# Sine table on ScalarE's queue, rotary queries first and query splits ahead of value rows in the opening of a latent attention, with a new order of its second list

## The chip, the cores and the metric

One NeuronCore of a Trainium2 chip. The metric is device time in microseconds (us) of one execution, the median of several runs. The engines are TensorE (PE in the profile), VectorE (DVE), ScalarE (ACT), GpSimd (POOL) and SyncE (SP). PEclk is the share of TensorE's full clock that was granted.

## The reference

One step of a hybrid encoder layer for two groups of rows, a prompt (1024) and a sample (32, with 512 cached rows), all in float32. What matters here is branch A, the multi-head latent attention of the prompt: 8 heads, 64 + 32 columns a head for scores.

```python
q = (rms_norm(q_lat, g_q_lat) @ w_uq).reshape(B, T, H_A, NOPE + ROPE)
q_nope = q[..., :NOPE]
q_rope = apply_rope(q[..., NOPE:], cos[:, None, :], sin[:, None, :])
k_nope, v = (c_kv @ w_uk), (c_kv @ w_uv)              # per head
s = (einsum(q_nope, k_nope) + einsum(q_rope, k_rope)) * MLA_SCALE
p = softmax(where(chunk mask, s, NEG))
o_a = einsum(p, v)
merged = sigmoid(g_a) * (o_a @ w_proj_a) + sigmoid(g_b) * (o_b @ w_proj_b)
```

Here `apply_rope` is `concat(x1 * cos - x2 * sin, x2 * cos + x1 * sin)`. `o_b` is the result of branch B (stick-breaking attention), which is done by the time this stage runs.

## The kernel before

Each float32 product is three matmuls on split operands: a tile `X` is held as an upper part (`hi`, L68, on ScalarE: `XH`, or `wh` of a weight) and a remainder (`lo`, L71, on VectorE: `XL`, `wl`), and `mm3` (L75 to L77) forms H·H + L·H + H·L. So nearly every operand of TensorE passes ScalarE first and VectorE second.

The stages follow one another: the combined projection, branch B, the latents (`stage_lat`, to about 572 us), the latent attention (`stage_mla`, to about 850), the merge, the feed-forward. `stage_mla` handles heads in four pairs. A list of tokens, `ORDER_M` for pairs 0 and 1 and `ORDER_N` for pairs 2 and 3, is read by `mla_attend` and gives the order of PE, ScalarE and VectorE in code order. Tokens begin with 0 or 1, the pair within the list: `S` scores (L1612 to L1617, into one of three `s` banks of PSUM), `M`, `m`, `n` row maxima and their scaling (L954 to L959), `E` the exponential (L961), which frees the bank, `R`, `C`, `c` the division by the sum (L966 to L970), `T` transposes (L806), `h`, `v` their splits, `V` products with the values (L820), `o`, `p` the outputs. Other tokens are fillers without a dependence on the scores: `f` is one step (three matmuls) of `o_b @ w_proj_b` (`proj_b`), `G` its store, `U`, `W`, `w` load and split the next weight of that projection, `Y` a step of the sample's attention, `q`, `r` split the last pair's outputs. In the second list the `Y` steps end with transposes (L1787), copied to `os` on VectorE (L1792), stored by GpSimd (L1794) and loaded again by SyncE (L1666) for the merge, whose first matmuls need the split of that load.

The change is mostly in the opening of `stage_mla`, ahead of the first list. Its pieces, by the tokens of `expansion(0)`: `y` the keys' matmuls, `H g L b` their splits into KH and KL; `z` the matmuls of the rotary part of four heads' queries (`rotary`), `B` (`turned`) the product of one third of them with the cosine or sine table (L1476 on VectorE), and behind the last third a store to DRAM on SyncE (L1478: rqc, rqs); `x` the matmuls of the other 64 columns a head, `X` and `K` their copies into a query tile (L1495 on VectorE, L1493 on ScalarE), where the first `X` also issues the loads of the stored products into rows 64 to 127 of the two query tiles (`rows`, L1485 on SyncE); `J` and `j` the query splits QH (L68) and QL (L71), `Z` a copy of the sample's query columns (L1508, L1509). `vstep` gives the values, 12 matmuls a step, with their copies (L1552) and remainders on ScalarE and VectorE in turn. `proj["P"]` fetches four tiles of `o_b` on SyncE (L1826), `proj["O"]` splits them into ObH and ObL. `krope_out` writes out the rotated keys; the rope rows of the keys are split into rows 64 to 127 of KH and KL, and GpSimd copies them to the second head's tiles.

The two tables are loaded at the start of the stage by SyncE (L1417); the sine table's tile is named KSm.

Of the kernel before, what the change touches and what calls it, by code (L numbers as in the profile page):

```python
# [44 lines left out]
class K:  # L45
# [838 lines left out]
    ORDER_N = """  # L884
        0S0.1 0M0.1 0S0.0 0n0.1 f 0M0.0 0S1.1 W f 0E0.1 0S2.0b 0n0.0 0M1.1 0R0.1 0E0.0 f 0R0.0 0c0.0 0C0.1
        0M2.0b 0S2.0a 0T0.0 f 0n1.1 0E1.1 0M2.0a 0m2.0 f w G 0h0.0 0R1.1 f 0v0.0 0E2.0a 0S1.0 0M1.0 f 0E2.0b
        0n1.0 f 0S2.1a 0C1.1 0M2.1a W 0S2.1b f 0M2.1b G 0E1.0 0m2.1 f 0E2.1a f 0S3.0b 0M3.0b 0s2.0 0E2.1b 0R1.0
        w f 0c1.0 0S3.0a f 0M3.0a 0s2.1 0m3.0 0R2.1 0V0.0 0o0 0S3.1b 0M3.1b 0E3.0a 0E3.0b f 0p0 0D 0T1.0 0T1.1
        0R2.0 G 0S3.1a 0h1.1 0M3.1a 0v1.1 f 0m3.1 f 0C2.1 0c2.0 0S4.0b f 0h1.0 0M4.0b f 0v1.0 0E3.1b G 0V1.1
        0s3.0 0E3.1a 0S4.0a 0T2.2 f 0T2.1 0M4.0a 0V1.0 0h2.2 0v2.2 0R3.0 0m4.0 0h2.1 0S4.1b f 0M4.1b 0E4.0b G  # L890
        0o1 0T2.0 f 0p1 0S4.1a 0v2.1 0V2.2 f 0s3.1 0h2.0 f 0E4.0a 0R3.1 0v2.0 0s4.0 f 0C3.1 0V2.1 0c3.0 f 0R4.0
        0V2.0 0T3.2 0o2 0T3.3 G 0M4.1a f3 0m4.1 0h3.2 0p2 0S5.0a f 0h3.3 0E4.1b 0I 0v3.3 0T3.1 0E4.1a 0V3.3
        0S5.0b 0v3.2 0V3.2 0i f 0M5.0b 0h3.1 0c4.0 U f2 G 0T3.0 0M5.0a 0m5.0 0v3.1 0E5.0b 0S5.1b 0h3.0 0x 0s4.1
        0R4.1 0S5.1a 0E5.0a 0C4.1 0x 0x 0T4.3 0M5.1b W 0M5.1a 0V3.1 0v3.0 G 0S6.1 0m5.1 0s5.0 0X 0R5.0 0h4.3
        0E5.1b 0T4.2 0v4.3 w 0E5.1a 0x 0V3.0 0h4.2 0T4.1 U 0M6.1 0s5.1 0R5.1 0x 0K 0o3 0h4.1 0x 0v4.2 0C5.1 0p3
        0x 0v4.1 0c5.0 0x 0K 0n6.1 0x 0V4.3 0V4.2 0E6.1 0T4.0 0X 0S6.0 0K 0T5.2 0S7.0 0h4.0 0X 0y 0R6.1 0Z 0J 0Z
        0C6.1 0M6.0 0h5.2 0v4.0 0n6.0 0E6.0 0y 0j 0R6.0 0V4.1 0V4.0 0H 0T5.1 0M7.0 0o4 0h5.1 0v5.2 0n7.0 0T5.0
        0S7.1 0L 0p4 1S1.0 0h5.0 0V5.2 0v5.1 0c6.0 0M7.1 0g 0J 0E7.0 0v5.0 0b 1M1.0 0j 0n7.1 f 0V5.1 0V5.0 0R7.0
        0T6.1 0T6.0 0o5 0h6.1 1S0.0 0y f 0c7.0 0v6.1 f2 0y G f 0h6.0 0H 0g 0E7.1 W 1S0.1 f2 1n1.0 1E1.0 f 1S2.0b
        1Y G 0v6.0 0R7.1 0C7.1 1M0.1 0p5 0L 0V6.1 1M0.0 1n0.1 1n0.0 0T7.0 1E0.0 1Y 1E0.1 1S2.0a w 0h7.0 1M2.0b  # L900
        1Y 1M2.0a 1R0.0 1m2.0 0V6.0 1Y 1c0.0 1S1.1 0b 1R0.1 0o6 1M1.1 1E2.0b 1Y 1E2.0a 1C0.1 0p6 1S2.1b 0v7.0
        0V7.0 1n1.1 1Y 1R1.0 1T0.0 1M2.1b 1S2.1a f 1M2.1a 1E1.1 1R1.1 1Y 1s2.0 0o7 1h0.0 1m2.1 1E2.1b f 1c1.0
        0p7 1Y 1C1.1 1R2.0 1v0.0 1E2.1a 1s2.1 1Y 1V0.0 f 1c2.0 1o0 1T1.1 1R2.1 1h1.1 1T1.0 1Y f 1h1.0 1C2.1
        1S3.0b 1v1.1 f 1p0 1T2.1 1M3.0b 1S3.0a 1v1.0 1M3.0a G U 1m3.0 f 1h2.1 1V1.1 1S3.1a 1E3.0a 1V1.0 1E3.0b
        1Y 1S3.1b 1v2.1 1M3.1a 1T2.2 1h2.2 f2 1o1 1T2.0 1M3.1b 1v2.2 1m3.1 f 1E3.1a 1Y 1p1 1Y 1S4.0b 1E3.1b
        1s3.0 1s3.1 1S4.0a 1M4.0b 1Y 1h2.0 f 1R3.0 1M4.0a 1Y 1c3.0 1q 1S4.1b 1V2.2 1M4.1b 1m4.0 1E4.0a 1Y 1E4.0b
        1R3.1 1Y 1v2.0 1S4.1a W 1C3.1 1Y 1M4.1a 1r 1m4.1 1T3.3 1q 1V2.1 1V2.0 1h3.3 1Y 1s4.0 1o2 1E4.1a 1R4.0
        1E4.1b 1Y 1v3.3 w 1T3.2 1h3.2 1r G 1s4.1 1R4.1 1p2 1Y 1v3.2 1T3.1 1V3.3 1V3.2 1T3.0 1c4.0 1h3.1 f 1Y
        1C4.1 f 1Y 1S5.0a 1S5.0b 1h3.0 1v3.1 1T4.3 1v3.0 1V3.1 1V3.0 1M5.0b 1M5.0a f 1q 1h4.3 1o3 1v4.3 1m5.0
        1T4.2 1S5.1b 1p3 1T4.1 1Y 1h4.2 1V4.3 1v4.2 1E5.0b 1h4.1 1S5.1a 1v4.1 1V4.2 1E5.0a 1M5.1b 1T4.0 1Y 1S6.1  # L910
        1h4.0 1M5.1a 1V4.1 1Y f 1m5.1 1s5.0 1M6.1 1r 1Y 1E5.1b G 1Y 1n6.1 1R5.0 1E5.1a 1s5.1 1v4.0 1c5.0 1S6.0
        1Y 1R5.1 1E6.1 1C5.1 1q 1M6.0 1T5.2 1R6.1 1Y 1n6.0 1h5.2 1V4.0 1C6.1 1r 1o4 f 1v5.2 1T5.1 1E6.0 1R6.0
        1h5.1 1p4 f 1v5.1 1T5.0 1S7.0 1c6.0 1M7.0 1n7.0 1S7.1 1V5.2 1h5.0 1v5.0 1T6.1 1V5.1 1q 1h6.1 1V5.0 G
        1M7.1 1v6.1 1o5 1T6.0 f 1E7.0 1h6.0 1n7.1 1Y 1r 1p5 1R7.0 1V6.1 1E7.1 1c7.0 f 1v6.0 1V6.0 1o6 1R7.1
        1C7.1 1T7.0 1h7.0 1p6 f3 1q 1v7.0 f G 1r 1q 1V7.0 f 1o7 1Y f 1p7 G 1r 1q 1r
    """.split()
# [493 lines left out]
    def stage_mla(self):  # L1410
# [4 lines left out]
        tc_, ts_ = M.tile([P, T], F32, name="tc", bufs=1), self.tl(M, [P, 2 * KS], F32, "KSm")[:, :T]  # L1415
        for x, d in zip((tc_, ts_), self.rtd):
            nc.sync.dma_start(x, d)  # L1417
# [7 lines left out]
        def expansion(p, banks="mm"):  # L1425
# [55 lines left out]
            def rows():  # L1481
                for e in range(2):
                    qf[e] = self.tl(self.At, [P, BIG], F32, "big")
                    for r, d in zip((64, 96), self.rqd):
                        nc.sync.dma_start(qf[e][r : r + 32], d[2 * p + e])  # L1485

# [327 lines left out]
    def proj_b(self, M, AB):  # L1814
# [6 lines left out]
        def fetch():  # L1821
            h = done[0] // 6
            for k in range(4):
                f = self.tl(self.At, [P, BIG], F32, "big") if h else self.tl(self.At, [P, TP], F32, "A")
# [1 line left out]
                self.fetched = nc.sync.dma_start(fs[-1], self.obd[k][:, h * HC : h * HC + HC]).ins  # L1826

# [878 lines left out]
```

## Time and profile before

| | us |
|---|---|
| median of 3 runs (lowest, highest) | 1706.3 (1703.85, 1706.9) |
| the profiled execution | 1706.11 |
| its span in the profile | 1704.3 |
| TensorE busy | 1648.0 |
| VectorE busy | 1268.7 |
| ScalarE busy | 1008.8 |

The profiled execution's own time and its span differ by 1.8 us. Rows of a timeline give the start in us from the span's start, the duration, engine, line, operation, out<-in with its tile, and in brackets the idle time before it and what ended it. SPq is SyncE's queue of DMA issues. A row of the windows gives, for a stretch, the busy time (and count) of PE, PEld (weight loads), DVE, ACT and POOL, then the granted clock, the DMA share and GB/s. A row of the waits gives who waited for what: total us, times, the longest.

### The profile page before, as it was taken

The numbers are of one execution on the slowest core, as the hardware profiler recorded it, in microseconds if no ns is written. First come the engines' busy times: TensorE is split into PE (matmuls) and PEld (weight loads), VectorE is DVE, ScalarE is ACT, GpSimd is POOL, SyncE is SP. The second block draws the span as 40 slices with busy tenths as digits, with TensorE's granted clock in tenths as the row PEclk, the third lists the DMA queues.
The fourth block names the chain that finished last, engine by engine and source line by source line (L and its number), as shares of the span: only waits on it lengthen the run. The fifth ranks groups of instructions, "written<-read, shape, count | busy, mean of one in ns | idle before, by whom it ended". The sixth has DMA issues, their size and how long they took to land. (4 is left out here: it accounts for less than half of the span.)

```text
span 1704.3 us, 30277 instructions
## 1 busy us (share of the span) xinstructions
PE 1648.0 (97%) x11592; PEld 1512.1 (89%) x11592; DVE 1268.7 (74%) x2140; ACT 1008.8 (59%) x1945; POOL 303.9 (18%) x581
## 2 busy tenths in 40 slices
...
GB/s 357 102 112 197 276 240 163 171 189 185 163 111 64 145 93 92 105 65 35 112 248 137 180 124 63 144 104 132 128 107 135 130 103 135 228 328 247 207 139 121
DMA packets 194145, 260.62 MB, mean 153 GB/s; under 512 B 23374, under 2 KB 132304, under 8 KB 193936
## 3 DMA queue, kind: packets, MB, share of 16 engines
...
q10 hardware_dynamic: 224, 0.09, 0.0%
...
## 5 line engine op out<-in xcount | busy, mean ns | idle before, releaser
L68 ACT ACTIVATE wh<-wr 128x1024 fp32r<-128x1024 f32 (+3 forms) x151 | 130.2, 864 | 231.4 <-PE s L2160 85.4
L71 DVE TENSOR_TENSOR wl<-wr,wh 128x1024 fp32r<-128x1024 f32 (+3 forms) x151 | 148.3, 985 | 78.9 <-ACT wh L68 76.2
L75 PE MATMUL mm<-hh,wh 128*128 128x352 f32 x456 | 152.3, 334 | 0.1
L76 PE MATMUL mm<-hl,wh 128*128 128x352 f32 x456 | 148.0, 325 | 0.2
L77 PE MATMUL mm<-hh,wl 128*128 128x352 f32 x456 | 148.0, 324 | 0.0
L2159 PE MATMUL mm<-T,wh 128*128 128x256 f32 (+1 forms) x376 | 108.1, 288 | 0.0
L2161 PE MATMUL mm<-T,wl 128*128 128x256 f32 (+1 forms) x376 | 107.1, 285 | 0.4 <-DVE wl L71 0.2
L2160 PE MATMUL mm<-T,wh 128*128 128x256 f32 (+1 forms) x376 | 106.6, 284 | 0.0
L2161 PE MATMUL s<-T,wl 128*128 128x256 f32 (+1 forms) x348 | 99.3, 285 | 0.0
L2159 PE MATMUL s<-T,wh 128*128 128x256 f32 (+1 forms) x348 | 99.3, 285 | 0.0
L2160 PE MATMUL s<-T,wh 128*128 128x256 f32 (+1 forms) x348 | 98.8, 284 | 0.0
L71 DVE TENSOR_TENSOR wl<-S,wh 128x1024 fp32r<-128x1024 f32 (+1 forms) x55 | 59.1, 1077 | 50.3 <-ACT wh L68 49.9
L75 PEld LDWEIGHTS mm<-hh,wh 128*128 128x128 f32 x456 | 86.3, 189 | 3.8 <-issue 2.1
L2300 DVE SCALAR_TENSOR_TENSOR u<-u,c,u 128x1058 f32<-128x1058 f32 x68 | 87.0, 1317 | 2.0 <-ACT u L2297 0.7
L76 PEld LDWEIGHTS mm<-hl,wh 128*128 128x128 f32 x456 | 86.2, 189 | 2.3 <-DVE hl L333 0.8
L806 PE MATMUL tr<-c,A 128*128 128x128 f32 x576 | 86.9, 273 | 0.2 <-DVE mx L959 0.2
L77 PEld LDWEIGHTS mm<-hh,wl 128*128 128x128 f32 x456 | 86.0, 189 | 0.6 <-issue 0.4
L68 ACT ACTIVATE wh<-S 128x1024 fp32r<-128x1024 f32 (+1 forms) x55 | 51.8, 943 | 48.2 <-PE s L2160 13.3
L2159 PE MATMUL tr<-T,wh 128*128 128x272 f32 (+1 forms) x272 | 77.8, 286 | 0.0
L2161 PE MATMUL tr<-T,wl 128*128 128x272 f32 (+1 forms) x272 | 77.6, 285 | 0.0
L2160 PE MATMUL tr<-T,wh 128*128 128x272 f32 (+1 forms) x272 | 77.3, 284 | 0.0
L806 PEld LDWEIGHTS tr<-c,A 128*128 128x128 f32 x576 | 69.3, 140 | 3.9 <-PE tr L806 0.4
...
## 6 DMA issues: line engine op xcount, KB each, us to landing
...
```

What stands on the lines that cost most here:

```text
L68: self.nc.scalar.activation(out, in_, AF.Identity, scale=scale)
L71: return self.nc.vector.tensor_tensor(out, full, hi.bitcast(F32), ALU.subtract)
L75: m(ps, lh, rh, start=start, stop=False)
L76: m(ps, lh, rl, start=False, stop=False)
L77: self.pe = m(ps, ll, rh, start=False, stop=stop).ins
L806: self.nc.tensor.transpose(tr[:, (2 * s + q) * P : (2 * s + q + 1) * P], at[q][:, b * P : b * P + P], self.idt)
L2159: m(ps[:, :n], w[0][:, k], x[0][:, k, c], start=first and k == 0, stop=False, skip_group_check=True)
L2160: m(ps[:, :n], w[0][:, k], x[1][:, k, c], start=False, stop=False, skip_group_check=True)
L2161: i = m(ps[:, :n], w[1][:, k], x[0][:, k, c], start=False, stop=k == 3, skip_group_check=True)
L2300: nc.vector.scalar_tensor_tensor(y, u[:, w : w + YW], self.cvT[:, w, cc : cc + 1], y, ALU.mult, ALU.add)
```

## The change

It has five parts. The sine table's load moves from SyncE's queue to ScalarE's. Three tile kinds become wider in memory (592 columns for `ptd`, 32 more for `lt`), without more use, so that the sine table's tile lies over others than before. The fetch of `o_b` moves from ahead of the opening into `operands` and is put behind the loads of the turned queries. The opening's token string starts with the rotary matmuls and their products; one value step, the query splits and the key's rope rows come ahead of the other value steps and the splits of `o_b`. And the second list, `ORDER_N`, is written in another order, with the same tokens.

```diff
     ORDER_N = """
-        0S0.1 0M0.1 0S0.0 0n0.1 f 0M0.0 0S1.1 W f 0E0.1 0S2.0b 0n0.0 0M1.1 0R0.1 0E0.0 f 0R0.0 0c0.0 0C0.1
+        0S0.1 0S0.0 f 0M0.1 0n0.1 0M0.0 0E0.1 0n0.0 0S1.1 f 0M1.1 0E0.0 0R0.1 W 0R0.0 0S2.0a 0c0.0 f 0n1.1 f
...
-    def diagonals(self, pool):
-        self.PTd = [[pool.tile([P, 512], F32R, name=self.nm("ptd"), bufs=1) for _ in range(2)]]
+    def diagonals(self, pool, n=512):
+        self.PTd = [[pool.tile([P, n], F32R, name=self.nm("ptd"), bufs=1)[:, :512] for _ in range(2)]]
...
-            x = self.tl(lp, [P, T], F32, "lt")
+            x = self.tl(lp, [P, T + 32], F32, "lt")[:, :T]
...
-        for x, d in zip((tc_, ts_), self.rtd):
-            nc.sync.dma_start(x, d)
+        nc.sync.dma_start(tc_, self.rtd[0])
+        nc.scalar.dma_start(ts_, self.rtd[1])
...
-        self.diagonals(M)
+        self.diagonals(M, 592)
...
-                        nc.sync.dma_start(qf[e][r : r + 32], d[2 * p + e])
+                        self.rq = nc.sync.dma_start(qf[e][r : r + 32], d[2 * p + e]).ins
...
-        proj["P"]()
...
-            for k in "yyHgLbyyHgLbzzzzzzzzzBBBBBBxxxXKxxxXKxxxXK":
+            for k in "zzzBBzzzBBzzzBByyHgLbyyHgLbxxxXKxxxXKxxxXK":
                 steps[k]()
-            ob = proj["O"]()
-            for _ in vstep:
-                next(ob)
-            self.krope_out()
-            proj["W"]()
-            proj["w"]()
+            next(vstep)
+            for k in "JjJj":
+                steps[k]()
             self.hi(KHs[0][64:128], self.KRp[64:128])
             self.lo(KLs[0][64:128], self.KRp[64:128], KHs[0][64:128])
             for x in (KHs, KLs):
                 nc.gpsimd.dma_start(x[1][64:128], x[0][64:128])
-            for k in "JjJjZZ":
+            ob = proj["O"]()
+            next(ob)
+            for _ in vstep:
+                next(ob)
+            self.krope_out()
+            for k in "ZZ":
                 steps[k]()
+            proj["W"]()
+            proj["w"]()
...
-                self.fetched = nc.sync.dma_start(fs[-1], self.obd[k][:, h * HC : h * HC + HC]).ins
+                with self.tc.issue_after(self.rq):
+                    self.fetched = nc.sync.dma_start(fs[-1], self.obd[k][:, h * HC : h * HC + HC]).ins
```

SyncE's queue at the opening, before (A<-ob are the fetches of `o_b`, of which two of four are shown):

```order
L1387 DMA A_6222<-big_6852 16x232
L1417 DMA KSm_6977<-rts 128x1056
L1826 DMA A_6995<-ob_2181 128x528
...
L1826 DMA A_7001<-ob_2184 128x528
L1478 DMA rqc<-VSm_7076 128x1056
L1478 DMA rqs<-big_7077 128x1056
L1485 DMA big_7096<-rqc 32x1056
```

And the same place in the change:

```order
L1387 DMA A_6222<-big_6852 16x232
L1478 DMA rqc<-VSm_7026 128x1056
L1478 DMA rqs<-big_7027 128x1056
L1485 DMA big_7088<-rqc 32x1056
...
L1830 DMA A_7151<-ob_2181 128x528
...
L1830 DMA A_7157<-ob_2184 128x528
```

The table has left the queue, and the four fetches stand behind the loads of the turned queries. VectorE at the end of the opening, before (the second splits of V and ObL belong to the last value step, `wl_6994` to the first weight of the projection, `mx` to the first list's row maxima):

```order
L71 TENSOR_TENSOR V_7017<-mm_7187,V_7017 128x4x64
L71 TENSOR_TENSOR ObL_7129<-A_7001,ObH_7128 128x528
L71 TENSOR_TENSOR wl_6994<-wr_7018,wh_6993 128x512
L71 TENSOR_TENSOR KL_6988<-A_6222,KH_6987 64x1024
L71 TENSOR_TENSOR QL_7228<-big_7096,QH_7226 128x1024
L71 TENSOR_TENSOR QL_7232<-big_7099,QH_7230 128x1024
L1508 COPY QZ_6223<-big_7096 64x32
...
L954 TENSOR_REDUCE mx_7244<-s_7246 128x1
```

In the change, first the piece with the query splits, then, after other value steps, the end:

```order
L71 TENSOR_TENSOR V_7009<-mm_7120,V_7009 128x4x64
L71 TENSOR_TENSOR QL_7139<-big_7088,QH_7137 128x1024
L71 TENSOR_TENSOR QL_7143<-big_7091,QH_7141 128x1024
L71 TENSOR_TENSOR KL_6988<-A_6222,KH_6987 64x1024
L71 TENSOR_TENSOR ObL_7150<-A_7151,ObH_7149 128x528
...
L71 TENSOR_TENSOR wl_6992<-wr_7012,wh_6991 128x1024
L71 TENSOR_TENSOR V_7009<-mm_7199,V_7009 128x4x64
L71 TENSOR_TENSOR ObL_7150<-A_7157,ObH_7149 128x528
L1508 COPY QZ_6223<-big_7088 64x32
...
L71 TENSOR_TENSOR wl_6994<-wr_7010,wh_6993 128x512
```

QL and KL have moved ahead of all four ObL, and the split of the projection's first weight, `wl_6994`, behind the second weight's and behind the copies of the sample's columns. VectorE round the sample's copy (`os`, L1792 before, L1795 after) at the end of the second list, before:

```order
L71 TENSOR_TENSOR PTl_10411<-tr_10405,PTh_10410 128x512
L966 RECIPROCAL sum_10371<-sum_10371 128x1
L968 TENSOR_SCALAR A_10369<-A_10369,sum_10371 128x256
L794 TENSOR_TENSOR o_10442<-pv_10427,o_10442 64x256
L71 TENSOR_TENSOR ptd_6983<-tr_10446,ptd_6982 128x384
L71 TENSOR_TENSOR V_9596<-o_10403,V_9596 64x256
L1792 COPY os_9715<-tr_10419 64x64 x2
```

And in the change:

```order
L71 TENSOR_TENSOR V_9594<-o_10339,V_9594 64x256
L71 TENSOR_TENSOR wl_10520<-KSm_10514,wh_10519 128x512
L71 TENSOR_TENSOR ptd_6983<-tr_10423,ptd_6982 128x384
L794 TENSOR_TENSOR o_10445<-pv_10418,o_10445 64x256
L71 TENSOR_TENSOR V_9594<-o_10404,V_9594 64x256
L1795 COPY os_9745<-tr_10448 64x64 x2
```

The transposes that the copy reads (`tr_10419`, `tr_10448`) stand on TensorE ahead of the products that feed `o_10442` before, and behind the products that feed `o_10445` in the change.

More of the change, by code (lines that the diff above doesn't have):

```diff
@@ L890 @@
[L890 to L904, printed above, removed]
@@ L915 @@
-        1C7.1 1T7.0 1h7.0 1p6 f3 1q 1v7.0 f G 1r 1q 1V7.0 f 1o7 1Y f 1p7 G 1r 1q 1r
+        0S0.1 0S0.0 f 0M0.1 0n0.1 0M0.0 0E0.1 0n0.0 0S1.1 f 0M1.1 0E0.0 0R0.1 W 0R0.0 0S2.0a 0c0.0 f 0n1.1 f
+        0C0.1 0E1.1 0S2.0b f 0T0.0 0M2.0a f 0M2.0b 0S1.0 0m2.0 G w 0E2.0a 0S2.1a 0E2.0b 0S2.1b 0D f 0M1.0 0R1.1
+        f 0n1.0 0h0.0 0E1.0 0s2.0 0v0.0 0M2.1b 0R1.0 0M2.1a 0m2.1 0c1.0 0V0.0 0C1.1 G 0S3.0a 0M3.0a f2 0E2.1b
+        0E2.1a 0T1.0 0S3.0b 0o0 0T1.1 f 0s2.1 0M3.0b 0h1.1 f 0m3.0 0R2.1 0R2.0 0p0 f 0h1.0 0E3.0b 0v1.1 0S3.1a f
@@ new lines @@
+        0S3.1b 0C2.1 f 0M3.1a 0c2.0 0M3.1b 0v1.0 0E3.0a f 0s3.0 G 0T2.0 0h2.0 0m3.1 0S4.0a 0E3.1a 0E3.1b 0v2.0 G
+        f 0V1.1 0S4.0b 0T2.2 0M4.0a 0h2.2 f 0V1.0 0M4.0b 0T2.1 0m4.0 0o1 0h2.1 f 0p1 0s3.1 f 0S4.1a 0R3.0 f G
+        0R3.1 0E4.0b f 0C3.1 0v2.1 0E4.0a 0v2.2 0c3.0 0M4.1a 0s4.0 0S5.0a 0S4.1b 0M4.1b f2 0V2.2 0T3.3 0m4.1 0I
+        0M5.0a 0E4.1a 0V2.1 0T3.2 0h3.3 0i 0S5.0b 0V2.0 0v3.3 0M5.0b 0h3.2 G 0E4.1b 0x 0m5.0 0x 0v3.2 0T3.1 0o2
+        0s4.1 0h3.1 0p2 0S5.1b 0R4.0 0x 0V3.3 U 0R4.1 0V3.2 0E5.0a 0c4.0 0v3.1 0T3.0 0C4.1 0S5.1a 0h3.0 0M5.1b
@@ new lines @@
+        0X 0M5.1a 0m5.1 0v3.0 0x 0T4.3 0E5.0b W 0E5.1b 0S6.0 0x 0h4.3 0M6.0 w 0n6.0 0v4.3 0E5.1a 0s5.0 0x 0K
+        0V3.1 0V3.0 0T4.2 0X 0x 0s5.1 0R5.0 0T4.1 0o3 0p3 U 0x 0h4.2 0E6.0 0h4.1 0V4.3 0R5.1 0x 0v4.2 0K 0R6.0
+        0V4.2 0T4.0 0C5.1 0v4.1 0S7.1 0S6.1 0X 0Z 0K 0h4.0 0c5.0 0V4.1 0T5.2 0Z 0J 0v4.0 f 0h5.2 f 0V4.0 f 0M7.1
+        0n7.1 f 0M6.1 0E7.1 0j 0o4 0R7.1 0n6.1 0T5.1 G 0y 0p4 0y 0C7.1 0h5.1 0v5.2 0E6.1 0H 0v5.1 0R6.1 0C6.1
+        0T5.0 f 0S7.0 0V5.2 0L 0h5.0 0J 1S0.0 0c6.0 f3 0T6.1 0M7.0 0g 0v5.0 0n7.0 0V5.1 0V5.0 0T6.0 1M0.0 0j 0b
@@ new lines @@
+        G 1S0.1 1n0.0 W 0h6.1 0E7.0 w 0R7.0 0o5 f 0c7.0 0v6.1 1M0.1 0y 0y f2 0h6.0 0p5 1n0.1 f 0V6.1 1S1.0 0T7.0
+        1E0.1 W 0v6.0 1E0.0 1S2.0b 1S1.1 G 0h7.0 0V6.0 f 0H f2 0g f 1Y 1M1.0 1R0.1 0v7.0 1n1.0 1M1.1 1R0.0 1E1.0
+        1c0.0 0o6 1Y 0L 1C0.1 1n1.1 1S2.0a 1R1.0 0p6 0V7.0 w 1E1.1 G 1Y 1M2.0b 1T0.0 1R1.1 1Y 0o7 1S2.1b f
+        1M2.0a 1Y 1m2.0 1h0.0 1E2.0b 1c1.0 0p7 1M2.1b 1C1.1 1E2.0a 1v0.0 U 1S2.1a 1M2.1a 1s2.0 1V0.0 f 1Y 1T1.1
+        1o0 1Y 1m2.1 1E2.1b 0b 1p0 1h1.1 1v1.1 1E2.1a 1s2.1 1T1.0 1R2.1 1h1.0 1R2.0 1C2.1 1Y 1V1.1 1v1.0 1c2.0
@@ new lines @@
+        1T2.1 1S3.0a 1h2.1 1T2.2 f 1Y 1V1.0 1v2.1 1Y f 1S3.0b 1T2.0 1M3.0a f 1Y f 1M3.0b 1m3.0 1h2.2 1o1 1S3.1a
+        1v2.2 W 1q 1p1 1E3.0a 1E3.0b 1S3.1b 1Y 1M3.1a 1S4.0b 1V2.2 G 1M3.1b 1Y 1s3.0 1m3.1 1M4.0b 1Y 1V2.1
+        1E3.1b 1Y 1R3.0 1S4.0a 1r 1h2.0 1v2.0 1E3.1a 1Y 1s3.1 1R3.1 1q 1M4.0a w 1C3.1 1c3.0 1Y 1m4.0 1S4.1b
+        1T3.3 1E4.0a 1h3.3 1Y 1E4.0b 1M4.1b 1v3.3 1Y 1S4.1a 1V2.0 1T3.1 1Y 1M4.1a 1s4.0 1m4.1 1h3.1 1E4.1a 1o2
+        1v3.1 1r 1T3.2 1p2 1Y 1V3.3 1h3.2 1v3.2 1V3.2 1T3.0 1E4.1b f 1V3.1 1s4.1 1R4.0 1R4.1 1c4.0 1h3.0 1S5.0a
```

21 lines of the change are left out of this document (7 added, 14 removed).

## The prediction

> **What bounds the kernel now.** I read the page first, then TensorE's waits, then the windows round the stage that the change touches, then each engine's timeline there.
>
> ```profile
> span 1704.3 us, 30277 instructions
> PE 1648.0 (97%) x11592; PEld 1512.1 (89%) x11592; DVE 1268.7 (74%) x2140; ACT 1008.8 (59%) x1945; POOL 303.9 (18%) x581
> PE s L1612 <- ACT QH L68: 8.2, 1, 8.2
> PE mm L75 <- ACT KH L68: 4.6, 1, 4.6
> PE s L75 <- DVE big L1476: 1.4, 1, 1.4
> 593.00:606.00 13.00, 4.20 (x18) 2.97 (x17) 10.14 (x20) 7.61 (x15) 5.41 (x9) 0.70 0.24 53
> 606.00:640.00 34.00, 34.00 (x237) 31.89 (x237) 26.56 (x70) 25.63 (x63) 4.92 (x9) 0.96 0.37 107
> 722.00:740.00 18.00, 15.97 (x103) 14.43 (x102) 13.80 (x40) 14.17 (x36) 2.21 (x4) 0.91 0.29 89
> 780.00:800.00 20.00, 20.00 (x129) 17.49 (x128) 15.21 (x42) 14.21 (x37) 2.72 (x5) 0.93 0.14 37
> ```
>
> TensorE is busy 97% of the span, so work on other engines is worth only the idle time it leaves TensorE, and the slow clock behind such idle time. The waits (total, times, longest) put the largest one in this stage: 8.2 us for QH, ScalarE's upper part of the rotated queries. In the window 593 to 606 TensorE works 4.2 of 13 us, while VectorE works 10.14. No matmul is removed or added, so the sum is about gaps alone. Now the chain that ends in QH, on SyncE, VectorE, ScalarE and TensorE:
>
> ```profile
> 575.61 2.47 SPq L1387 DMA_DIRECT2D A<-big  x4
> 578.18 0.52 SPq L1417 DMA_DIRECT2D KSm<-rts  x1
> 578.80 3.75 SPq L1826 DMA_DIRECT2D A<-ob  x4
> 585.35 0.32 SPq L1478 DMA_DIRECT2D rqc<-VSm  x1
> 590.27 0.41 SPq L1485 DMA_DIRECT2D big<-rqs  x1
> A<-ob SPq DMA_DIRECT2D x4, 264.0 KB, 4.1
> 583.51 0.52 DVE L1476 TENSOR_TENSOR big<-s,KSm 128x352 f32<-128x352 f32 x1 [4.93 <-DMA KSm<-rts]
> 569.43 0.42 ACT L1237 ACTIVATE A<-A 128x264 f32<-128x264 f32 x1
> 589.50 0.46 ACT L1493 ACTIVATE big<-s 64x352 f32<-64x352 f32 x1 [12.90 <-DMA rqs<-big]
> 599.51 1.05 ACT L68 ACTIVATE KH<-A 64x1024 fp32r<-64x1024 f32 x1
> 600.59 2.00 ACT L68 ACTIVATE QH<-big 128x1024 fp32r<-128x1024 f32 x2
> 601.70 0.58 PE L1612 MATMUL s<-KH,QH 128*128 128x256 f32 x1 [8.24 <-ACT QH L68]
> ```
>
> The sine table (KSm) is issued by SyncE at 578.18, behind four small loads, and VectorE needs it at 583.51, 5.33 us later. The products with it are stored (585.35) and read back turned (last issue 590.27). ScalarE waits 12.90 us for that store, then does values and splits, and QH last.
>
> **The change part by part.** *Sine table on ScalarE's queue.* ScalarE is free at 569.43 + 0.42 = 569.9 and has nothing until the keys. With the 5.33 us seen above the table is there at 575.2 instead of 583.5. Its wider neighbours (padding) only let it start; they cost no work. The issue on ScalarE's queue is not in the trace: SyncE's is 0.52, so I take 0.5, hidden in that idle stretch.
>
> *Rotary queries first.* The same matmuls in another order.
>
> ```profile
> 575.20 0.32 PE L75 MATMUL s<-lat,wh 128*128 128x352 f32 x1
> 579.56 0.32 PE L75 MATMUL s<-lat,wh 128*128 128x352 f32 x1
> ```
>
> The 27 rotary matmuls take 579.56 − 575.20 = 4.36 us. Started at 572.3 they end at 576.7, so VectorE's six products can end at about 577.6. Behind the first of the four small loads SyncE is held until 578.08 as now (the row at 575.61), so the store is issued at 578.1 instead of 585.35: 7.25 us earlier. The read back then runs from 580.8 to 583.0. The value fetches (ob), now behind it on the same queue, take 583.4 to 587.2, and land 4.1 us later, at 587.5 to 591.3; before they were never late. TensorE's wait of 1.4 us for a product (L1476) goes, but that only lets it wait longer for what follows.
>
> *Query splits ahead of value rows.* The read back lands by about 586.4. QH takes 2.00 to 588.4, the key's rope rows 1.05 to 589.5. Behind them VectorE has QL and KL:
>
> ```profile
> 591.98 0.42 DVE L71 TENSOR_TENSOR V<-mm,V 128x256 fp32r<-128x256 f32 x1 [0.45 <-ACT V L1552]
> 592.52 0.71 DVE L71 TENSOR_TENSOR ObL<-A,ObH 128x528 fp32r<-128x528 f32 x1
> 593.14 0.42 DVE L71 TENSOR_TENSOR V<-s,V 128x256 fp32r<-128x256 f32 x1
> 600.60 1.22 DVE L71 TENSOR_TENSOR KL<-A,KH 64x1024 fp32r<-64x1024 f32 x1 [0.39 <-ACT KH L68]
> 601.85 2.36 DVE L71 TENSOR_TENSOR QL<-big,QH 128x1024 fp32r<-128x1024 f32 x2
> 604.13 0.17 DVE L1508 COPY QZ<-big 64x32 f32<-64x32 f32 x1
> 604.94 0.42 DVE L954 TENSOR_REDUCE mx<-s 128x1 f32<-128x256 f32 x1
> 606.15 0.29 DVE L954 TENSOR_REDUCE mx<-s 128x1 f32<-128x128 f32 x1 [0.60 <-PE s L1617]
> 606.55 0.68 DVE L954 TENSOR_REDUCE mx<-s 128x1 f32<-128x512 f32 x1
> 607.35 1.22 DVE L71 TENSOR_TENSOR wl<-wr,wh 128x1024 fp32r<-128x1024 f32 x1
> 605.91 0.42 PE L75 MATMUL mm<-ObH,wh 128*128 128x264 f32 x1
> 610.01 0.34 PE L1612 MATMUL s<-KH,QH 128*128 128x384 f32 x1
> ```
>
> QL from 587.5, the second QH's half behind it, ends at 589.8, and KL at 591.0. The first score's matmuls thus begin about 589.5 (601.70 before), 12 us earlier, and end with KL. That is the whole gain if nothing else is late. **But something is:** eight projection steps (f, at 605.91 before) follow the first three scores on TensorE, and they need the last ObL and wl. These are now *behind* QL and KL on VectorE, where before they were ahead of them. From 591.0 VectorE has: four ObL at 593.14 − 592.52 = 0.62, 2.5 us; six value remainders of 0.42, 2.5; three maxima with their scaling, 0.42 + 0.16, 606.55 − 606.15 = 0.40 and 607.35 − 606.55 = 0.80, 1.8; wl of 1024 columns, 1.2; four copies, 604.94 − 604.13 = 0.8; wl of 512, half of that of 1024, 0.6. That is 9.4 us and a little waiting, so f is fed at **600.6 instead of 605.9: 5.3 us gained**, and TensorE idles most of the time from 591 to 600. Bounds: each V that waits for ScalarE costs 0.45 (row at 591.98); three more such pairs give 1.4 us, so 601.9 and 4 gained; VectorE's rows overlap by some 0.07 each, some 20 rows, so 599.1 and 6.8.
>
> The clock behind the gap: the window 606 to 640 shows a granted 0.96, 34 x 0.04 = 1.4 us lost. After the change TensorE is as cold at f, so I take the same; lost twice (scores at 589.5 and f apart) it costs 1.4 more, not lost at all it gives 1.4. From the end of the eight f's (610.01) on, the first list is unchanged in order, and TensorE has no gap in it before 720; so the 5.3 is carried through (3 to 8).
>
> *The second list.* Its stretch begins near 722. Its gaps, now:
>
> ```profile
> 724.42 0.50 PE L1612 MATMUL s<-KH,QH 128*128 128x320 f32 x1 [2.03 <-ACT A L961]
> 778.28 0.39 PE L1612 MATMUL s<-KH,QH 128*128 128x256 f32 x1 [1.61 <-ACT A L961]
> 837.64 0.41 PE L75 MATMUL s<-QH,wh 128*128 128x352 f32 x1
> 841.92 0.46 DVE L1792 COPY os<-tr 64x64 f32<-64x64 f32 x2
> 849.77 0.95 PE L75 MATMUL mm<-KH,wh 128*128 128x352 f32 x2 [4.63 <-ACT KH L68]
> ```
>
> At the start the same score waits for the same exponential; a weight split moves behind it, but its scaling comes behind one more remainder of V: 0.4 us lost. At the turn to the last head pair the score that waits 1.61 us now follows an earlier exponential, but a weight split stands between them on ScalarE: between 3 us gained (its wait of 1.6 and the clock behind it, 20 x 0.07 = 1.4) and 2 lost, 0.5 taken. At the end the sample rows' last transposes end at 837.64, VectorE copies them only at 841.92 (4.28 later, behind pieces that wait for ScalarE), and the merge starts at 849.77, a chain of 12.1 us, under which TensorE has 7.5 us of work and then waits 4.63. In the new list fewer pieces stand ahead of that copy: I take 0.75 us, so a chain of 8.6; TensorE's work behind the transposes is 5.7. Gap 2.9: 1.7 gained (0 to 2.5). The list together: 1.8, from −4 to +5, since its hundreds of other places are new too, and any could wait.
>
> The Trainium skill (TensorE: Matmul & The Clock Gate, "Why this matters for your kernels") asks for no idle gap over about 3 us, one window, or the clock drops. The trace disagrees on size: the gaps of 2.03 and 1.61 us are followed by granted clocks of 0.91 and 0.93. By the page the turn's gap would cost its 1.6 alone, the turn would lie between 1.6 gained and 2 lost, and the sum would be 0.7 us less; by the rows it is as above.
>
> **Sum:** 5.3 + 1.8 = 7.1 us. From the profiled 1706.11 us (span 1704.3 and 1.8 around it) that is 1699.0; the median shown is 0.2 higher, so **1699.2**.
>
> **The rivals.** *The f's are not late* (0.15). If ScalarE and VectorE overlap much better than in the rows, TensorE keeps the 12 us from 601.70 to 589.5, and the list adds its 1.8: about 1693. For it: VectorE idles before 591. Against: its queue above is full.
>
> *The gain is eaten* (0.20): f at 602, cold twice, and the list 2 us worse: 4 − 1.4 − 2, about 1705.5. For it: ScalarE's and VectorE's turns show 0.45 waits; against, VectorE has no more work than before.
>
> *Slower by a list that runs dry* (0.10). Place: the turn of the second list to the last head pair, where scores wait for a bank that an exponential behind a weight split releases. Price: 2.03 + 18 x 0.09 = 3.6 us a wait. The opening's 5.3 and the end's 1.7 are lost with two such waits; four give 1706.3 − 7 + 14.4, some 1714. It decides from the third on (10.8 − 7 is above the 3.4 below). For it: TensorE has no gap from 740 to 776 now, ScalarE and VectorE being three quarters busy. Against: the list holds the same instructions.
>
> *The table isn't early* (0.05). If it waits for what it overwrites and lands at 583 as now, the opening ends 8 us later than above, f at 608.6: 2.7 us slower, with the list's 1.8 about 1707.
>
> **How the numbers follow.** The forecast has 0.50 (1695.5 to 1702.5 from its bounds). 0.2% is 3.4 us, about what a measurement of this kernel can tell from no change. Faster by over that: the forecast, the first rival, a little of the second: 0.66. Within it: most of the second, the table: 0.23. Slower: 0.11. The range reaches from the first rival, 1693, to the second with its bad end, 1706.5; left out are the dry list, the late table's worse half and some of the first rival's lower tail.
>
> **What would show it.** KSm lands near 575; the store (L1478) is issued by SyncE near 578; the waits of 8.2 for QH and 1.4 for the product are gone, and in their place a wait of f for VectorE's wl or ObL, of 4 us or more in one piece or several, with f near 600.6; no wait over 2.5 us near 775; the merge's wait near 3 us. The forecast is wrong if TensorE is full from 593 on, if f starts after 604, or if the second list shows waits that the old one has not.

## The result and the profile after

The changed kernel takes 1700.54 us (median of 7 runs, 1699.02 to 1703.29), before 1706.3 (7 runs). The ratio is 0.9969, with an interval of 0.9955 to 0.9982: 5.3 us faster (3.1 to 7.7). A second measurement of the same kernel (e12 below) gave 0.9964 (0.9951 to 0.9977). The forecast was 1699.2, 7.1 us faster.

Page of the changed kernel, and its longest wait in the second list (who waited for whom: total us, times, longest):

```profile
span 1698.8 us, 30285 instructions
PE 1647.6 (97%) x11592; PEld 1511.4 (89%) x11592; DVE 1269.9 (75%) x2140; ACT 1008.5 (59%) x1945; POOL 300.3 (18%) x581
```

```profile
PE s L1615 <- ACT A L961: 2.8, 1, 2.8
```

TensorE's work is the same to 0.4 us. The wait of 8.2 us for QH is gone, and in its place stand four waits in the opening, 1.22, 1.41, 4.34 and 1.09, together 8.1. That they lie earlier gains nothing by itself: before, TensorE also waited 1.45 us for the product with the sine table, 1.37 for ScalarE's copies of the queries (L1493) and 0.56 for QL, and these are gone. Up to the eighth f TensorE idled 11.6 us before and 8.1 in the change, and the difference, 3.6 us, is the opening's gain but for what the clock does. The windows (busy time of PE, PEld, DVE, ACT and POOL, granted clock, DMA share, GB/s) and TensorE's timeline show where:

```profile
593.00:606.00 13.00, 6.16 (x24) 5.01 (x24) 8.95 (x24) 5.97 (x16) 4.60 (x8) 0.58 0.36 82
606.00:640.00 34.00, 34.00 (x234) 31.32 (x232) 25.05 (x66) 25.40 (x61) 4.92 (x9) 0.96 0.33 100
720.00:740.00 20.00, 17.19 (x111) 15.33 (x110) 15.21 (x44) 14.54 (x38) 2.48 (x4) 0.91 0.21 67
780.00:800.00 20.00, 20.00 (x135) 17.00 (x134) 16.14 (x41) 16.18 (x41) 2.19 (x4) 1.00 0.12 34
```

```profile
572.81 0.63 PE L1375 MATMUL mm<-hl,wk 128*32 128x264 f32 x8
590.93 0.36 PE L1615 MATMUL s<-KH,QH 128*128 128x256 f32 x1
592.52 0.39 PE L1616 MATMUL s<-KL,QH 128*128 128x256 f32 x1 [1.22 <-DVE KL L71]
594.56 0.47 PE L1615 MATMUL s<-KH,QH 128*128 128x512 f32 x1 [1.41 <-DVE mx L959]
601.13 0.59 PE L75 MATMUL mm<-ObH,wh 128*128 128x264 f32 x1 [4.34 <-ACT wh L68]
603.03 0.59 PE L77 MATMUL mm<-ObH,wl 128*128 128x264 f32 x1 [1.09 <-DVE wl L71]
```

And TensorE before, up to the wait for QH that the prediction shows:

```profile
571.74 0.63 PE L1375 MATMUL mm<-hl,wk 128*32 128x264 f32 x8
584.08 0.43 PE L75 MATMUL s<-lat,wh 128*128 128x352 f32 x1 [1.45 <-DVE big L1476]
590.01 0.39 PE L75 MATMUL s<-wh,lat 128*128 128x256 f32 x1 [1.37 <-ACT big L1493]
```

The last matmuls of the stage before (L1375) start at 572.81 in the change and at 571.74 before: this execution came to the stage 1.07 us later. Ahead of that row the change has no more than the width of `lt`, and that isn't the cause: over the fourteen traces it lies between 570.3 and 573.2, and the three earliest (e1, e3, e4) have the wider tile. So all comparisons below count from that row. The table has, for each kernel, the starts on TensorE of: the first score, the first f, the score that follows the eighth f, the values of the second half (first matmul into a `tr` bank ahead of the second list) and the merge, less the start of that row. The last columns are the median time and the ratio to before.

| | first score | first f | after 8 f | second half | merge | us | ratio (interval) |
|---|---|---|---|---|---|---|---|
| before | 29.96 | 34.17 | 38.27 | 143.71 | 278.03 | 1706.3 | |
| change | 18.12 | 28.32 | 35.22 | 141.03 | 272.38 | 1700.54 | 0.9969 (0.9955 to 0.9982) |
| e12, change again | 18.12 | 28.10 | 34.05 | 139.46 | 272.35 | 1699.5 | 0.9964 (0.9951 to 0.9977) |
| e1, opening only | 18.12 | 27.80 | 34.05 | 139.47 | 272.79 | 1702.08 | 0.9976 (0.9967 to 0.9985) |
| e2, second list only | 29.13 | 33.35 | 37.64 | 143.08 | 276.04 | 1702.46 | 0.9979 (0.997 to 0.9988) |
| e3, table only | 27.57 | 31.78 | 35.51 | 140.93 | 274.03 | 1703.08 | 0.9983 (0.9974 to 0.9992) |
| e4, table on SyncE | 24.25 | 33.89 | 40.18 | 145.57 | 276.55 | 1706.14 | 1.0 (0.999 to 1.0011) |
| e5, early weight | 18.79 | 24.03 | 32.09 | 138.90 | 269.74 | 1698.88 | 0.9958 (0.9942 to 0.9974) |
| e6, early weight and o_b | 21.44 | 27.58 | 31.38 | 140.60 | 272.41 | 1701.66 | 0.9969 (0.9959 to 0.998) |
| e7, 18 idle matmuls | 18.11 | 28.14 | 35.05 | 141.03 | 271.27 | 1699.98 | 0.9965 (0.9952 to 0.9979) |
| e8, no padding | 18.12 | 27.85 | 34.04 | 139.43 | 270.98 | 1699.87 | 0.996 (0.9945 to 0.9975) |
| e9, 45 idle matmuls | 18.10 | 28.52 | 32.30 | 137.75 | 266.25 | 1695.32 | 0.994 (0.9929 to 0.9952) |
| e10, o_b behind the queries | 19.29 | 27.16 | 30.92 | 141.96 | 275.48 | 1699.86 | 0.9966 (0.9953 to 0.9979) |
| e11, and four f's first | 19.95 | 21.85 | 32.40 | 138.89 | 272.57 | 1697.39 | 0.9951 (0.9939 to 0.9963) |

The first score is 11.84 us earlier than before. After the eighth f 3.05 of that are left, at the second half 2.68, at the merge 5.65. There is one trace of each kernel, of a single execution, and small differences between them mean little: e2 has the opening of before, yet its first score is 0.83 us earlier, since the wait for the product with the table was 0.74 us there for 1.45. Some of the traced executions also lie off their kernel's median: e1's took 1699.58 us, e4's 1703.33, e10's 1704.56.

How the table, SyncE's queue, VectorE and ScalarE went in the opening of the changed kernel, and its rows round the merge:

```profile
570.51 0.36 ACTq L1417 DMA_DIRECT2D KSm<-rts  x1
575.57 0.51 DVE L1476 TENSOR_TENSOR big<-mm,KSm 128x352 f32<-128x352 f32 x1
576.85 3.25 SPq L1387 DMA_DIRECT2D A<-big  x4
580.20 0.53 SPq L1478 DMA_DIRECT2D rqc<-VSm  x1
593.99 0.42 DVE L71 TENSOR_TENSOR V<-s,V 128x256 fp32r<-128x256 f32 x1
596.83 0.29 DVE L954 TENSOR_REDUCE mx<-s 128x1 f32<-128x128 f32 x1 [1.26 <-PE s L1620]
599.23 0.38 ACT L1552 ACTIVATE V<-mm 128x256 fp32r<-128x256 f32 x1 [1.89 <-DVE V L71]
600.45 0.62 ACT L68 ACTIVATE wh<-wr 128x512 fp32r<-128x512 f32 x1
602.28 0.69 DVE L71 TENSOR_TENSOR wl<-wr,wh 128x512 fp32r<-128x512 f32 x1
836.00 1.00 PE L1790 MATMUL tr<-big,big 128*128 128x64 f32 x8
837.59 0.46 DVE L1795 COPY os<-tr 64x64 f32<-64x64 f32 x2
845.19 0.59 PE L75 MATMUL mm<-KH,wh 128*128 128x352 f32 x2 [2.67 <-ACT KH L68]
```

The table costs no wait any more. The store (L1478) follows the four small loads at once. VectorE's last split for f, wl, ends near 603, and f's third matmul starts with it. f's first matmul waits for ScalarE's wh, and ScalarE is late with it because it stood 1.89 us for a remainder of V on VectorE.

### The profile page after: what moved, and what is told of

It reads as the page before. It is cut to its first block, busy times and chain, and to the rows that moved or that the text cites. A ratio compares the mean times of both kernels' runs of the same rounds, so it can differ in the third digit from the quotient of the medians.

```text
span 1698.8 us, 30285 instructions
## 1 busy us (share of the span) xinstructions
PE 1647.6 (97%) x11592; PEld 1511.4 (89%) x11592; DVE 1269.9 (75%) x2140; ACT 1008.5 (59%) x1945; POOL 300.3 (18%) x581
## 5 line engine op out<-in xcount | busy, mean ns | idle before, releaser
L68 ACT ACTIVATE wh<-wr 128x1024 fp32r<-128x1024 f32 (+2 forms) x151 | 130.2, 864 | 228.7 <-PE s L2164 85.8
L71 DVE TENSOR_TENSOR wl<-wr,wh 128x1024 fp32r<-128x1024 f32 (+2 forms) x151 | 148.3, 985 | 79.4 <-ACT wh L68 79.0
L71 DVE TENSOR_TENSOR PTl<-tr,PTh 128x512 fp32r<-128x512 f32 x96 | 65.3, 685 | 12.0 <-ACT PTh L68 11.3
```

What stands on the lines that cost most here:

```text
L68: self.nc.scalar.activation(out, in_, AF.Identity, scale=scale)
L71: return self.nc.vector.tensor_tensor(out, full, hi.bitcast(F32), ALU.subtract)
```

## The experiments

Three theories stood for the whole. Theory 1: half of the opening's gain goes to the new wait of f, and the second list adds a part of its own. Theory 2: all comes from the list. Theory 3: all comes from the opening.

**e1, the opening without the new list.** The changed kernel with the old text of `ORDER_N`.

> The change without its new second list: the table, the padding and the new opening, with the old second list. Theory 1 (the new wait of the projection steps eats half of the opening's gain): 3 us under before (the eight f's ended 3.0 us earlier in the changed kernel's trace once its later start of 1.1 us is taken off), so a ratio near 0.998; in the trace the waits of TensorE for wh and wl (4.3 and 1.1) stay, and the old list's waits of 2.0, 1.6 and 4.6 are back. Theory 2 (all of the gain comes from the second list, since the opening's gap only moved): ratio 1.000 within 0.0005. Theory 3 (all of it from the opening): ratio 0.997.

Ratio 0.9976: 4.1 us (2.6 to 5.6), a little more than theory 1 said. The four waits of the opening are the same, and the old list's 4.6 is back.

**e2, the list alone.** Before, with the new `ORDER_N`.

> Before, with the new second list alone. Theory 1: 2.5 us under before, ratio 0.9985: the wait of 8.2 for QH stays, the waits in the second list are one near its start and one of 2.7 ahead of the merge. Theory 2: ratio 0.997. Theory 3: ratio 1.000.

Ratio 0.9979: 3.6 us (2.0 to 5.1). Theories 2 and 3 fall: each half has its part. The two together, 0.0045, lie within the interval of the change's second measurement, at the upper end of the first's. The traces place less in the list: from the second half to the merge the kernels with the old list took 134.32 us (before), 133.32 (e1) and 133.10 (e3), those with the new one 131.35 and 132.89 (the change), 132.96 (e2) and 130.98 (e4), on average 1.5 us less.

**e3, the table alone.** Before, with the padding and

```diff
-        for x, d in zip((tc_, ts_), self.rtd):
-            nc.sync.dma_start(x, d)
+        nc.sync.dma_start(tc_, self.rtd[0])
+        nc.scalar.dma_start(ts_, self.rtd[1])
```

> Before, with the sine table on ScalarE's queue and the padding, and the old order of the opening and of the list. The table is early, but the products with it still come behind the keys, and the fetches of o_b stand ahead of the store on SyncE. Theory 1: the wait of 1.4 for the product goes, the store is issued near 582 instead of 585.4, so QH is some 3 us earlier if the value and ObL splits ahead of it on ScalarE start earlier too: the wait for QH shrinks to 5 to 6 us, ratio 0.998. Rival (ScalarE and VectorE, not the table, set the time of QH): the wait for QH grows by what TensorE saved, ratio 1.000.

Ratio 0.9983: 2.9 us (1.4 to 4.4). In its waits and TensorE's timeline:

```profile
PE s L1612 <- ACT QH L68: 8.2, 1, 8.2
```

```profile
586.19 0.39 PE L75 MATMUL s<-wh,lat 128*128 128x256 f32 x1 [0.79 <-ACT big L1493]
```

The wait for QH has not shrunk: TensorE and ScalarE both came 2.4 us earlier (first score 27.57 for 29.96). My mark, a smaller wait, missed; the gain came all the same, from the waits ahead of it: the one of 1.45 us for the product is gone, and the one for L1493 is 0.79 us for 1.37. So the table alone brings most of what the whole opening brings (e1).

**e4, the table back on SyncE.** The changed kernel with `nc.sync.dma_start(ts_, self.rtd[1])`.

> The changed kernel with the sine table back on SyncE's queue, where it stands behind the four small loads as before. Theory 1: the table comes near 583 to 585, all of the opening behind it moves by 7 to 8 us, the f's start near 609: 6 to 7 us over the changed kernel, ratio to before 1.001. Rival (the order, not the table, brings the gain): ratio 0.997.

Ratio 1.0, as theory 1 said. SyncE and VectorE:

```profile
577.97 0.53 SPq L1417 DMA_DIRECT2D KSm<-rts  x1
581.66 0.52 DVE L1476 TENSOR_TENSOR big<-mm,KSm 128x352 f32<-128x352 f32 x1 [8.22 <-DMA KSm<-rts]
```

Without the early table the new order costs: in this trace TensorE idles 12.6 us up to the eighth f, 11.6 before, the second half starts 1.9 us later than before (145.57 for 143.71), and the list's gain pays for it. The padding was in this kernel; the table still stood behind the four small loads.

**e5, the weight of f first.** The changed kernel with `proj["W"]()` and `proj["w"]()` ahead of the opening's string, and the first weight in the unused half of its tile:

```diff
-            w.append([x[:, :n] for x in AB[i % 3 != 1]])
+            o = 512 if done[1] == 1 else 0
+            w.append([x[:, o : o + n] for x in AB[i % 3 != 1]])
```

> The changed kernel with the split of the projection's first weight (wh of 512 columns on ScalarE, wl on VectorE) done ahead of the opening, in the unused half of its tile. Theory 1 (f waits for VectorE's queue as a whole, its last pieces being the splits of o_b, the copies and wl): wl and its 0.69 and the copies' 1.0 are out of f's way, f's first full triple moves from 603.0 to about 601.3, when the last ObL ends: 1.5 to 2 us under the changed kernel, ratio to before 0.996. Rival (f waits for the weight alone): f is ready with the third score near 597, 6 us under, ratio 0.9935.

The ratio, 0.9958, is on theory 1's number, though its interval holds the change's. The timeline:

```profile
596.26 0.42 PE L75 MATMUL mm<-ObH,wh 128*128 128x264 f32 x1
598.59 0.59 PE L76 MATMUL mm<-ObL,wh 128*128 128x264 f32 x1 [0.58 <-DVE ObL L71]
601.07 0.59 PE L76 MATMUL mm<-ObL,wh 128*128 128x264 f32 x1 [0.61 <-DVE ObL L71]
```

f now starts right behind the third score, and then waits for one ObL after the other, and 0.47 us for an ObH. Both parts of VectorE's queue were in f's way, the weight and the splits of `o_b`. The matmuls between run at 0.22 us, the slow clock.

**e6, `o_b` early too.** As e5, with `proj["P"]()` ahead of the opening on ScalarE's queue and the four splits between the keys and `x`.

> As the run with the early weight, and the four tiles of o_b are fetched on ScalarE's queue right behind the sine table and split behind the keys, ahead of the query splits. Theory 1: nothing that f needs is left behind QL and KL, TensorE goes from the third score (596.8) straight to f, with no wait for wh or wl; f starts some 6 us earlier than its full triple in the changed kernel, 4 to 6 us under it, ratio to before 0.994. Rival (ScalarE's and VectorE's total work up to the first scores sets the time, so QH and KL come later by what was moved ahead of them): the first score comes 3 to 5 us later, ratio 0.997 as the change itself.

Ratio 0.9969, as the rival said. The first score is 3.3 us later than the change's, and f has no wait left; then TensorE waits for the first rows' division. TensorE and ScalarE:

```profile
570.91 10.52 ACTq L1833 DMA_DIRECT2D A<-ob  x4
581.48 1.20 ACT L68 ACTIVATE KH<-mm 64x512 fp32r<-64x512 f32 x2 [10.60 <-DMA A<-big]
594.21 0.39 PE L1618 MATMUL s<-KH,QH 128*128 128x256 f32 x1 [1.68 <-ACT KH L68]
608.57 0.38 ACT L1881 COPY nat<-mm 128x264 f32<-128x264 f32 x1 [4.10 <-DMA out_dram<-nat]
609.30 0.69 PE L806 MATMUL tr<-c,A 128*128 128x128 f32 x2 [2.09 <-ACT A L970]
```

The rival's reason, more work ahead of QH and KL, is not all. The issues of the four fetches take ScalarE's own queue up to 581.43, and its first key split starts 2.1 us later than in the change (581.48 − 572.77 against 579.44 − 572.81). And the division (L970) stands on ScalarE behind the copy of f's second result into a store tile (`nat`), which waits 4.10 us for a DMA: by the profile for GpSimd's store of the rotated keys (`krope_out`), which are held in such a tile too.

**e10 and e11, `o_b` behind the queries.** As e5, with all four splits of `o_b` right behind the query and key splits; in e11 the first list also begins `0S0.1 0M0.1 0n0.1 f4 0S1.1 0E0.1 0S0.0 W f ...`.

> The changed kernel with the early weight and the four splits of o_b right behind the query and key splits, ahead of the remaining value steps. Theory 1 (the order on VectorE sets when TensorE can go on, and something has to be last): f's operands are ready near 595, but the second score, whose bank waits for a value remainder, is now about 2 us later, f's follow it near 598 without further waits: equal to the run with the early weight alone within 1 us, ratio 0.995 to 0.996. Rival (f's operands alone): 3 us under that run, ratio 0.9935.

> As e10, and the first list begins with four f's right behind its first score, ahead of the second. Theory 1: the f's fill the time that the second score's bank needs, TensorE has only gaps under 1 us between 592 and 606, 5 us under the changed kernel at its end of the eighth f; the clock may take 1 to 2 back: ratio 0.9935 to 0.995. Rival (the values' end on VectorE, not f, is the bound): as e10.

e10 gave 0.9966, no better than the change, though its interval holds theory 1's number. The second score, which waits for a remainder of V, is 2.9 us later than in the change (24.62 for 21.75 from the common row), f follows without a wait, and the first division again holds TensorE, behind the same copy:

```profile
596.44 0.77 PE L1615 MATMUL s<-KH,QH 128*128 128x512 f32 x1 [3.27 <-DVE V L71]
607.74 0.38 ACT L1878 COPY nat<-mm 128x264 f32<-128x264 f32 x1 [4.56 <-DMA out_dram<-nat]
608.47 0.69 PE L806 MATMUL tr<-c,A 128*128 128x128 f32 x2 [2.67 <-ACT A L970]
```

e11 gave 0.9951, with f 6.5 us earlier than the change (21.85 for 28.32) but only 0.6 to 2.1 left at the second half. The gaps weren't all under 1 us, as theory 1 said: 1.05 for KL and 1.60 for a remainder of V were left, and the copy waited 3.54 us for the store. So e6, e10 and e11 show that f's operands alone don't bound the opening. What is brought forward on ScalarE and VectorE pushes another piece back, the first score in e6 and e11 (21.44 and 19.95 for 18.12 from the common row) and the second in e10; and behind f stands a limit that is no work of either engine, the store of the rotated keys. What that store costs stays open: no run here gave the copy another tile.

**e7 and e9, TensorE kept busy.** The changed kernel with matmuls into a bank that nothing reads, 18 or 45 of them, between the third score and the first f. They compute nothing that is used. The cut shows e7; e9 has 45 in place of 18, and the list's line goes on where the dots stand.

```diff
+                elif k == "A":
+                    ps = self.bank("pv")
+                    for _ in range(18):
+                        nc.tensor.matmul(ps[:, :256], QHs[0][0][:, :P], KHs[0][:, :256], start=True, stop=True)
...
-        0S0.1 0M0.1 0n0.1 0S1.1 0E0.1 0S0.0 f4 W f ...
+        0S0.1 0M0.1 0n0.1 0S1.1 0E0.1 0S0.0 A f4 W f ...
```

> The changed kernel with 18 matmuls of 256 columns more, on the first score's operands into a bank of PSUM that nothing reads, between the third score and the first f, so that TensorE works through its wait of 4.3 us. It computes nothing in addition. Theory (a part of the opening's gain goes to the slow clock behind the gap): the eight f's run at 0.12 us a matmul from about 603 instead of 0.22, so they end 2 us earlier, ratio to before 0.9955 to 0.996. Rival (the clock does not depend on that gap): the same as the changed kernel or up to 1 us over it.

> As the run with 18 extra matmuls, but with 45, so that TensorE is busy from the third score until f's weight is split, without the gaps of 1.2 and 1.4 us that were left. Theory (a gap of under 1.5 us, following others, is enough to bring the slow clock back): now the eight f's run at 0.12 us a matmul from about 603 and end about 606 instead of 608, 2 us before the changed kernel, ratio to before 0.9955. Rival (the slow stretch has another cause than idle time): f's at 0.22 still, ratio 0.997.

With 18 nothing was won. The extra matmuls end near 600, and two gaps are left:

```profile
596.37 3.35 PE L1634 MATMUL pv<-KH,QH 128*128 128x256 f32 x18
600.92 0.39 PE L75 MATMUL mm<-ObH,wh 128*128 128x264 f32 x1 [1.19 <-ACT wh L68]
601.14 0.28 PE L76 MATMUL mm<-ObL,wh 128*128 128x264 f32 x1
602.82 0.59 PE L77 MATMUL mm<-ObH,wl 128*128 128x264 f32 x1 [1.39 <-DVE wl L71]
```

The matmul at 601.14 takes 0.28, full speed; behind the gap of 1.39 each takes 0.42, until about 608. The score that follows the eighth f starts at 35.05, no earlier than in the change. With 45:

```profile
595.91 5.56 PE L1634 MATMUL pv<-KH,QH 128*128 128x256 f32 x45
602.32 0.39 PE L77 MATMUL mm<-ObH,wl 128*128 128x264 f32 x1 [0.61 <-DVE wl L71]
602.54 0.28 PE L75 MATMUL mm<-ObH,wh 128*128 128x264 f32 x1
```

And its window at the second list's start:

```profile
720.00:740.00 20.00, 20.00 (x142) 17.80 (x141) 15.68 (x42) 17.00 (x43) 4.46 (x7) 1.00 0.20 58
```

No f is slow, the score that follows the eighth starts 1.75 to 2.9 us earlier than in the two traces of the change (32.30 for 34.05 and 35.22), and the ratio is 0.994: some 4 us less than the change's 0.9964 from the same runs of before. Not all of that is shown to be the extra matmuls' doing. In this trace the clock was back in the third score, ahead of them (0.28 us for the matmul at 595.55; 0.42 for the same one, at 595.92, in the change); they then kept it. And a part is won behind the opening, where the second list's first wait is 1.24 us for 2.81, its first stretch has full clock (1.00 from 720 to 740, 0.91 in the change) and the merge is 6 us earlier. That wait follows one of ScalarE for the last tile of `o_b`'s second half, in the change and in e9:

```profile
718.59 0.64 ACT L68 ACTIVATE ObH<-big 128x528 fp32r<-128x528 f32 x1 [2.22 <-DMA big<-ob]
713.77 0.65 ACT L68 ACTIVATE ObH<-big 128x528 fp32r<-128x528 f32 x1 [0.69 <-DMA big<-ob]
```

SyncE issues that fetch 0.1 us behind the first values of the second half in both (713.97 and 710.68), and ScalarE goes on 4.6 us later in the change, 3.1 in e9. Nothing here shows that the extra matmuls made the tile land sooner. Of all kernels here e9 has the lowest median, and it does more work than any other.

**e8, without the padding.** The changed kernel with `diagonals(M)` and the narrow `lt`.

> The changed kernel without the padding: the table on ScalarE's queue, but its tile again over the one that the key's rope matmuls read until 572.8. Theory 1: the issue waits for those matmuls, some 2 us more than the changed kernel, the store of the products moves by as much, but it was held by the four small loads for part of it: 1 us over the changed kernel, ratio 0.9975. Rival (padding matters most, the issue waits for more than these matmuls): the table near 583, ratio 1.000.

Ratio 0.996, not slower than the change. ScalarE, VectorE and SyncE:

```profile
572.66 0.36 ACTq L1417 DMA_DIRECT2D KSm<-rts  x1
576.19 0.52 DVE L1476 TENSOR_TENSOR big<-mm,KSm 128x352 f32<-128x352 f32 x1 [1.37 <-DMA KSm<-rts]
579.25 0.53 SPq L1478 DMA_DIRECT2D rqc<-VSm  x1
```

The issue comes when the last rope matmuls end (571.97 + 0.63), 3.0 us later than in the change counted from their start, and VectorE waits 1.37 us for the table. But the store comes 7.28 us after the last L1375 (579.25 − 571.97), 7.39 in the change (580.20 − 572.81): it is the four small loads, issued up to 579.15, that hold it. The padding moves a wait that lies beside another one. The 1 us that I expected from it does not show.

**e12, the change again.**

> The changed kernel once more, for a second trace and a narrower interval: ratio 0.9965 to 0.9975. If the stretch of slow clock behind f is a matter of where the gap falls, not of the program, the granted clock between 603 and 610 and the end of the eighth f may differ from the first trace by 1 us while all starts up to f agree within 0.3.

Starts up to f agree within 0.22 us, and the score after the eighth f differs by 1.17. Its window behind f, for 0.96 in the first trace:

```profile
606.00:640.00 34.00, 34.00 (x243) 31.45 (x242) 26.20 (x70) 25.74 (x62) 4.92 (x9) 1.00 0.37 113
```

## Why the prediction was right, and where its sizes were off

Right were the sign, the place and the mechanism: the first score 12 us earlier (11.84), most of it given back in a wait of f for the last splits on VectorE, and a smaller wait ahead of the merge. By the profile the longer of f's two waits, 4.34 us, ends with ScalarE's wh; but ScalarE came late to it by its own wait for VectorE (the row at 599.23), and VectorE had no gap from 596.83 on until wl was done. By its steps, with 1.1 us taken off the changed kernel's times for its later start:

- *The table early.* Forecast: no longer late, store 7.25 us earlier. Right in size: 6.2 us (580.20 − 1.07 against 585.35). The small loads that hold SyncE took 3.25 us, not 2.47. e4 shows that without the early table nothing is won, and its 1706.1 is near the price that the rival "the table isn't early" gave (about 1707). The padding, which I said lets the load start, was not needed for the time (e8).
- *Query splits first.* QL and KL end where the working put them: KL's first user starts at 592.52 − 1.07 = 591.5 (forecast 591.0).
- *f fed at 600.6.* It was 603.03 − 1.07 = 602.0, 1.4 late and just past the bad end of the bounds (601.9); it is the 602 of the rival "the gain is eaten", without that rival's other two terms. The step that failed is the sum of VectorE's queue without a wait. Its work was as counted: from the first ObL at 592.50 to the end of wl at 602.97 are 10.5 us, 9.2 without the wait, for 9.4 forecast. But VectorE stood 1.26 us for the third score's maximum (the row at 596.83), because the second score had waited 1.41 us for its bank. That the bank was freed by the remainder of V at 593.99 is my reading: the profile ends the wait with the scaling of the first maximum, which ends 0.07 us behind that remainder, and in e10 it puts the second score's wait down to V itself. I had counted the V that waits for ScalarE, not TensorE waiting for V and VectorE for TensorE in turn.
- *The clock behind it.* I took the same loss as before. TensorE was at half speed over all eight f's in the first trace (5 us from the third matmul on, where before it took 4.1 for all), and for five of them in e12. That is 1 us in the one, nothing in the other. e1 and e8, with the same opening, have that score at 34.05 and 34.04 as e12 has, so the first trace is the odd one.
- *Opening, sum.* 5.3 forecast. In the traces 3.05 and 4.22 at the score behind the eighth f, 2.68 and 4.25 at the second half; 4.1 by time (e1). f itself was fed 3.9 us earlier than it started before (602.0 for 605.9).
- *The second list.* 1.8 forecast, 3.6 by time (e2, 2.0 to 5.1), 1.5 by the traces (see e2). The merge's gap is 2.67 (2.9 forecast): the copy of the sample rows starts 0.6 us behind the end of the transposes (837.59, transposes to 837.0; 0.75 forecast). The turn to the last head pair has no wait left, the good end of its range, and the clock there is 1.00 from 780 to 800 for 0.93. That part of the clock isn't the list's: e1 and e3 have the old list and the same wait of 1.61 us, and the 20 us behind it are granted 1.00 in both. The list's first wait is 2.81 for 2.03. Of these 0.8 us the list has the 0.4 that I took: the score goes on 0.6 us longer than ScalarE's wait for the tile of `o_b` (2.81 and 2.22; 2.99 and 2.39 in e12), with the old list 0.2 longer (2.03 and 1.84; 2.05 and 1.85 in e1). The rest is that tile, which landed later. New waits of 0.61 and 0.68 at 816.68 and 833.59 are the places I could not work out.

So by the traces the opening gave 3.1 to 4.2 us for 5.3 and the list 1.5 for 1.8, and 5.3 for 7.1 in all fits that. The times of e1 and e2 alone add up to 7.7, more than either measurement of the whole (5.3 and 6.1); their intervals allow the smaller figures too.

What stays open: how the 4.1 of e1 splits between the table (e3, 2.9) and the order on top of it; their intervals overlap. The traces of e1 and e3 give the order 1.5 us at the second half (139.47 for 140.93); with the change's first trace, 141.03, it is nothing.
